# A two-layer decoder trunk on one core: a list scheduler that knows of the DVE/POOL lock, and elementwise work moved from GpSimd to VectorE

## The chip, the core and the metric

The kernel runs on one core of a Trainium2 chip. The engines are named as the profile names them: PE (TensorE; PEld its weight loads), DVE (VectorE), ACT (ScalarE), POOL (GpSimd) and SP (the queue that issues the DMAs). The metric is the device time of one execution in microseconds. The time before is the median of three runs.

## What is computed

`reference()` is a trunk of two layers over 512 tokens of width 1024, all in float32. `c` conditions it: six vectors per layer (shift, scale and gate of the token mixing, then of the MLP) come from one product of `silu(c)` with `w_ada`.

```python
for l in range(DEPTH):
    mod = (ada_in @ w_ada[l] + b_ada[l])[:, None, :]
    sh1, sc1, g1, sh2, sc2, g2 = jnp.split(mod, 6, axis=-1)
    h = x * (1.0 + sc1) + sh1
    proj = h @ w_in[l]
    ...
    o_h = hgrn2(...)          # gated recurrence, 4 heads of 64
    o_n = nsa(...)            # sparse attention, 8 heads in 2 groups
    o_g = gmlp(...)           # chunked spatial gating
    mix = jnp.concatenate([o_h, o_n, o_g], axis=-1) @ w_o[l]
    x = layer_norm(DN_ALPHA * x + (1.0 + g1) * mix, ln1_w[l], ln1_b[l])
    h = x * (1.0 + sc2) + sh2
    y = jnp.square(jax.nn.relu(h @ w_ff1[l])) @ w_ff2[l]
    x = layer_norm(DN_ALPHA * x + (1.0 + g2) * y, ln2_w[l], ln2_b[l])
```

## The kernel before

**Products.** PE multiplies float32 numbers as pairs of rounded float32r parts: each operand is split into a high part (a rounding copy, `whi`) and a low part (the difference, `wlo`), and each product is three matmuls (`mm3`). So every weight tile that a DMA brings (`raw`) costs a copy and a subtraction on ACT, DVE or POOL (`split`), and so does each input tile `hT` (`make_hT`: PE transposes a normalised tile, ACT or DVE multiplies by the scale and adds the shift, then a cast and a difference of 128x256).

**The stretches, by the trace's time.** Layer 0: input projections with the conditioning vectors (0 to 73); gated recurrence, query, key and value projections (73 to 180); compressed keys, attention and the remaining projections (180 to 320); output projection and residual (320 to 398); norm and the MLP's input (398 to 426); MLP (426 to 780); norm and the next layer's input (780 to 808). Layer 1 is the same: recurrence and projections (808 to 920), attention (920 to 1040), output projection (1040 to 1124), norm (1124 to 1152), MLP and end (from 1152).

**Norms.** `layer_norm_rows` gathers statistics on DVE, takes the reciprocal root with two small POOL instructions (`rsqrt`, tile `lnmv`) and normalises in place on DVE. The norm's own weight and bias are folded into the columns `sb` with which `make_hT` makes the next input; the affine rows themselves are needed only much later, as the residual. `affine_rows` (L1623) makes them: per half of the columns and token tile a product and a sum of 128x512 on engine `E`, then a DMA to a scratch tensor `xd`. It is called three times, after ln1 and ln2 of layer 0 and ln1 of layer 1, with `E = G`, which is POOL.

**Conditioning vectors.** `ada_accs` (L906) accumulates `silu(c)[k] * w_ada[k]` over eight k tiles from 512 KB loads. On DVE a step is one fused multiply-add (`scalar_tensor_tensor`); on POOL it is a product into a tile `adat` and a sum. `rest(m, dst, eng)` (L1778) makes the gate `g1` (`ada_row`, two halves) and then shift and scale `sb2` of the MLP (`ada_scale_shift`). Layer 0's are made on POOL (`eng = "G"`), layer 1's on DVE.

**Order.** The program is first written down as a list of operations on virtual tiles. `Plan.schedule` (L332) then places them one by one: per engine a queue of ready operations in order of priority (place in the list plus `plan.shift`), a cost in ns for each (`cost`, L218), latencies between engines, a limited number of tiles of each kind. Many operations have alternatives: `vg` (L765), a product, sum or difference, may go to DVE or, if it has been ready for 500 ns, to POOL; `split` and copies may go to ACT or DVE. The instructions are emitted in the order in which they were placed; engines work through their own instructions in that order. In the trace all instructions have the emitting line, L563, and the tiles of the common pool are all called `t`.

Of the kernel before, what the change touches and what calls it, by code (L numbers as in the profile page):

```python
# [36 lines left out]
# ---------------------------------------------------------------- planning  # L37
# Instructions are first written down with virtual tiles, then placed in time by a
# list scheduler with a rough cost of each instruction, and emitted in that order.
# [117 lines left out]
class Op:  # L157
    __slots__ = ("ahead", "alts", "prio", "seq", "reads", "writes", "succ", "nd", "ready", "vts", "newv", "eng", "end",
# [6 lines left out]
NFILL = 1  # L165
STEPS = (1, 1, 2, 2, 2)
# [22 lines left out]
class Plan:  # L189
# [17 lines left out]
    def limit(self, name, n):  # L207
        """at most n tiles of this name live at once"""
        self.add_class("#" + name, n, 0, None)
        self.lims[name] = "#" + name  # L210
# [6 lines left out]
    # ---- cost in ns  # L217
    def cost(self, eng, method, a, k):  # L218
# [4 lines left out]
        if eng == "PE":  # L223
# [3 lines left out]
            if a[2].dt == F32:  # L227
                return max(2 * n / 2.4, a[1].idx.size / 1.2) + 2 * n / 2.4 + 2.5
            return n / 2.4 + 2.5
# [27 lines left out]
        return 100.0  # L257

    def op(self, alts, also=()):
# [56 lines left out]
        o.nd = len(deps)  # L316
        o.succ = []
# [13 lines left out]
    # ---- placement in time  # L331
    def schedule(self):  # L332
# [7 lines left out]
               "SP": dict(PE=100.0, V=0.0, A=0.0, G=0.0, SP=0.0)}  # L340
        table = None
# [32 lines left out]
        def slot_time(o, t):  # L374
            """earliest time at which the new tiles of o can have slots; INF: not known yet"""
# [29 lines left out]

        for o in self.ops:
            if o.nd == 0:
                push(o)
# [6 lines left out]
        while n_left:  # L415
            best = None
            for e in T:
# [14 lines left out]
                for r in sorted(ready[e])[:200]:  # L432
# [3 lines left out]
                    st = max(slot_time(o, t), bank_time(o, e))  # L436
# [14 lines left out]
                if cand is None:  # L451
                    for r in pend[e]:
# [5 lines left out]
                        fut = min(fut, max(r[0] + (ALT_WAIT if r[2] else 0), slot_time(o, r[0]), bank_time(o, e)))  # L458
# [13 lines left out]
            start = t  # L472
            if e == "PE":
                load = 0.0
                if alt[1] == "matmul":
                    load = alt[2][1].idx.size / (2.4 if alt[2][1].dt == BF else 1.2)
# [30 lines left out]
            if e == "SP":  # L507
# [4 lines left out]
                dma_free = tr + nbytes / 350.0  # L512
                end = dma_free + 950
                T[e] = start + 460
            else:
                end = start + c
                T[e] = end
            o.done = True
# [25 lines left out]
    def place(self, vt):  # L544
        pool, width = self.classes[vt.cls]["pool"], self.classes[vt.cls]["width"]
        n = int(np.prod(vt.shape[1:]))
        t = pool.tile([128, width], vt.dt, name="%s_%d" % (vt.cls, vt.slot), tag="%s%d" % (vt.cls, vt.slot))
# [19 lines left out]
def trunk(ctx: ExitStack, tc: tile.TileContext, I, out, depth=L):  # L567
# [44 lines left out]
    # ------------------------------------------------------------ constants  # L612
# [12 lines left out]
    # ---- condition vector and the bias of its projection, as columns  # L625
# [1214 lines left out]
```

## Time and profile before

| | us |
|---|---|
| median of three runs | 1514.28 |
| lowest, highest | 1511.14, 1516.61 |
| span of the profiled execution | 1509.3 |
| PE busy (share) | 1376.6 (91%) |
| DVE busy | 1170.3 (78%) |
| ACT, POOL busy | 554.9, 462.4 |
| mean granted PE clock | 0.971 |

The span runs from the first to the last instruction of one profiled execution; the median of the runs, taken without the profiler, is 5.0 us above it. Busy time of DVE and POOL counts an instruction from its start to its end, with what it waits for in between at a port. The chain of waits that ended last is 64% PE and 25% DVE.

### The profile page before, as it was taken

The numbers are of one execution on the slowest core, as the hardware profiler recorded it, in microseconds if no ns is written. First come the engines' busy times: TensorE is split into PE (matmuls) and PEld (weight loads), VectorE is DVE, ScalarE is ACT, GpSimd is POOL, SyncE is SP. The second block draws the span as 40 slices with busy tenths as digits, with TensorE's granted clock in tenths as the row PEclk, the third lists the DMA queues.
The fourth block names the chain that finished last, engine by engine and source line by source line (L and its number), as shares of the span: only waits on it lengthen the run. The fifth ranks groups of instructions, "written<-read, shape, count | busy, mean of one in ns | idle before, by whom it ended". The sixth has DMA issues, their size and how long they took to land.

```text
span 1509.3 us, 21620 instructions
## 1 busy us (share of the span) xinstructions
PE 1376.6 (91%) x7459; PEld 1151.8 (76%) x7459; DVE 1170.3 (78%) x2477; ACT 554.9 (37%) x1465; POOL 462.4 (31%) x601
## 2 busy tenths in 40 slices
PE   6867888999879999999998789999896999999996
PEld 4756777777768887888887769888785888888885
DVE  9999979999978557486789995999996663444658
ACT  6541567783203313122314344877421311101121
POOL 6676577453420001010036642223424000000003
PEclk9888999999989999999999899999999999999998
DMA  9521454225466325275414115111454331233331
GB/s 314 183 72 51 119 179 136 71 83 180 152 221 211 132 88 181 97 255 175 147 42 136 35 49 148 30 57 52 147 173 153 126 103 55 94 99 98 111 112 56
DMA packets 119845, 185.69 MB, mean 123 GB/s; under 512 B 9796, under 2 KB 47160, under 8 KB 119736
## 3 DMA queue, kind: packets, MB, share of 16 engines
q1 hardware_dynamic: 119736, 184.31, 38.1%
q8 instruction: 59, 0.97, 0.3%
q14 instruction: 50, 0.41, 0.1%
HBM read 175.89 MB, written 8.39 MB: 122 GB/s over the span
## 4 chain that ended last, share of the span: by engine, by line
PE 64%; DVE 25%; issue 4%; ACT 4%; POOL 2%; DMA 2%; SPq 0%; POOLq 0%; DVEq 0%; ACTq 0%
PE ps L563 64%; DVE t L563 21%; ACT t L563 3%; DVE amax L563 1%; POOL t L563 1%; DMA t<-in_w_ada_dram 1%; DMA raw<-in_w_ada_dram 1%; POOL lnmv L563 1%; DVE acoef L563 1%; DMA t<-in_ln_w_dram 0%; DVE hst L563 0%; POOL hms L563 0%; DVE lt L563 0%; DVE adat L563 0%; POOL gmv L563 0%
## 5 line engine op out<-in xcount | busy, mean ns | idle before, releaser
L563 PE MATMUL ps<-t,t 128*128 128x512 f32 (+5 forms) x6096 | 1261.7, 363 | 72.3 <-DVE t L563 67.2
L563 PEld LDWEIGHTS ps<-t,t 128*128 128x128 f32 x6096 | 1016.5, 193 | 251.8 <-DVE t L563 40.7
L563 ACT ACTIVATE t<-ps 128x512 f32<-128x512 f32 (+11 forms) x462 | 179.0, 413 | 539.9 <-PE ps L563 528.0
L563 POOL TENSOR_TENSOR t<-t,t 128x512 f32<-128x512 f32 (+5 forms) x244 | 241.4, 1004 | 255.4 <-ACT t L563 133.1
L563 DVE TENSOR_TENSOR t<-raw,t 128x512 fp32r<-128x512 f32 (+2 forms) x376 | 248.2, 678 | 13.7 <-ACT t L563 7.2
L563 POOL TENSOR_TENSOR t<-raw,t 128x512 fp32r<-128x512 f32 (+2 forms) x56 | 65.6, 1176 | 535.7 <-ACT t L563 368.5
L563 DVE TENSOR_TENSOR t<-t,t 128x512 fp32r<-128x512 f32 (+6 forms) x270 | 182.2, 694 | 5.9 <-ACT t L563 0.8
L563 DVE TENSOR_TENSOR t<-t 128x512 f32<-128x512 f32 (+1 forms) x94 | 60.1, 653 | 151.7 <-ACT t L563 151.6
L563 ACT ACTIVATE t<-raw 128x512 fp32r<-128x512 f32 (+2 forms) x241 | 128.4, 568 | 129.3 <-DMA raw<-in_w_ff_dram 107.5
L563 PE MATMUL ps<-ident,t 128*128 128x128 f32 (+1 forms) x635 | 110.7, 282 | 36.8 <-DVE t L563 20.4
L563 ACT ACTIVATE t<-t 128x512 fp32r<-128x512 f32 (+5 forms) x202 | 98.1, 510 | 112.0 <-DVE t L563 95.8
L563 PEld LDWEIGHTS ps<-ident,t 128*128 128x128 f32 (+1 forms) x635 | 75.9, 144 | 57.6 <-issue 18.3
L563 DVE TENSOR_TENSOR t<-ps,t 128x512 fp32r<-128x512 f32 (+5 forms) x237 | 109.3, 482 | 9.1 <-ACT t L563 3.9
L563 DVE SCALAR_TENSOR_TENSOR t<-raw,silc,t 128x512 f32<-128x512 f32 x98 | 74.6, 773 | 10.7 <-DMA raw<-in_w_ada_dram 9.4
L563 DVE CAST t<-raw 128x512 fp32r<-128x512 f32 (+2 forms) x191 | 81.4, 430 | 0.2
L563 ACT ACTIVATE t<-ps,amax 128x128 f32<-128x128 f32 (+3 forms) x128 | 67.3, 534 | 20.2 <-DVE amax L563 18.4
L563 DVE TENSOR_TENSOR t<-t,ps 128x512 f32<-128x512 f32 (+1 forms) x48 | 31.1, 650 | 53.7 <-PE ps L563 53.5
L563 DVE TENSOR_REDUCE amax<-ps 128x1 f32<-128x32 f32 (+4 forms) x192 | 65.5, 380 | 4.0 <-PE ps L563 3.1
L563 POOL TENSOR_SCALAR t<-t,acoef 128x384 f32<-128x384 f32 (+3 forms) x55 | 32.2, 599 | 67.6 <-DVE acoef L563 51.7
L563 ACT ACTIVATE t<-ps,adasb 128x256 f32<-128x256 f32 x48 | 23.4, 571 | 72.4 <-PE ps L563 72.4
L563 POOL TENSOR_SCALAR t<-raw,silc 128x512 f32<-128x512 f32 x48 | 37.3, 782 | 27.4 <-PE ps L563 9.9
L563 POOL TENSOR_SCALAR lnmv<-lnmv 128x1 f32<-128x1 f32 x16 | 5.6, 348 | 113.8 <-DVE lnmv L563 113.8
(141 smaller groups left out, 878.5 us busy)
## 6 DMA issues: line engine op xcount, KB each, us to landing
raw<-in_w_ff_dram SPq DMA_DIRECT2D x128, 512.0 KB, 4.5
raw<-in_w_ada_dram SPq DMA_DIRECT2D x80, 512.0 KB, 4.6
raw<-in_w_in_dram SPq DMA_DIRECT2D x49, 256.0 KB, 2.9
t<-in_w_ada_dram SPq DMA_DIRECT2D x32, 256.0 KB, 6.1
raw<-in_w_o_dram SPq DMA_DIRECT2D x16, 512.0 KB, 4.0
raw<-in_w_in_dram SPq DMA_DIRECT2D x15, 512.0 KB, 3.6
xd<-t SPq DMA_DIRECT2D x24, 256.0 KB, 2.2
t<-xd SPq DMA_DIRECT2D x24, 256.0 KB, 4.9
```

Of the source, the lines that this page charges most:

```text
L563: getattr(self.handles[e], method)(*a, **k)
```

## The change

Four things, one of which is the order that follows from the others.

1. The scheduler's `shares` says which instructions of DVE and POOL use the shared port of SBUF: on POOL all but memsets, on DVE those with two SBUF inputs, or with SBUF on both sides of a copy or a scalar operation. `port_time` lets such a DVE instruction start at the earliest 69 ns before the end of POOL's, and POOL's 147 ns before the end of DVE's.
2. Costs: a DVE instruction that needs news from several engines starts 62 ns later for each beyond the first; float32 and float32r matmuls and their weight loads are dearer; DMAs run at 310 instead of 350 bytes per ns.
3. Layer 0's `rest` goes to DVE (`"V"` for `"G"`).
4. `affine_rows` runs on DVE, and its priority is 900 places behind its place in the list, not 250.

Besides, tiles bear their own names in the changed program (`place`), and comments are gone.

```diff
+OPEN_V, OPEN_G = 69.0, 147.0
+WAIT = 62.0
...
             if a[2].dt == F32:
-                return max(2 * n / 2.4, a[1].idx.size / 1.2) + 2 * n / 2.4 + 2.5
-            return n / 2.4 + 2.5
+                return 2 * max(2 * n / 2.4 + 2.5, 111.0)
+            if a[2].dt == BF:
+                return n / 2.4 + 2.5
+            return n / 2.246 + 4.0
...
+    def shares(self, eng, method, a, k):
+
+        if eng == "G":
+            return method not in ("memset", "iota")
+        if eng != "V" or method == "memset":
+            return False
+        out = k.get("out", a[0] if a else None)
+        ins = [x for x in list(a[1:]) + [x for n, x in k.items() if n != "out"] if isinstance(x, VA)]
+        ins = [v for v in ins if v.vt.cls not in self.psum and (v.idx.size > 1 or out.idx.size == 1)]
+        if method in ("tensor_copy", "tensor_scalar"):
+            return bool(ins) and out.vt.cls not in self.psum
+        return len(ins) > 1
...
+        def port_time(o, ai, e):
+            if e not in port or not o.port[ai]:
+                return 0.0
+            return port["G"] - OPEN_V if e == "V" else port["V"] - OPEN_G
...
-                    st = max(slot_time(o, t), bank_time(o, e))
+                    st = max(slot_time(o, t), bank_time(o, e), port_time(o, r[2], e))
...
+            news = 0
+            last = {}
+            for d in o.deps:
+                x, i = d.eng_no
+                last[x] = max(last.get(x, -1), i)
+            for x, i in last.items():
+                if i > seen[e].get(x, -1):
+                    seen[e][x] = i
+                    news += 1
+            if e == "V" and news > 1:
+                start += WAIT * (news - 1)
...
-                    load = alt[2][1].idx.size / (2.4 if alt[2][1].dt == BF else 1.2)
+                    load = 4 + alt[2][1].idx.size / (2.4 if alt[2][1].dt == BF else 1.2)
...
-                dma_free = tr + nbytes / 350.0
+                dma_free = tr + nbytes / 310.0
...
+                if e in port and o.port[ai]:
+                    port[e] = end
...
-        r = layer(l, yn, xd, sb, rest(0, nxt, "G") if l == 0 else iter(()), nxt)
+        r = layer(l, yn, xd, sb, rest(0, nxt, "V") if l == 0 else iter(()), nxt)
         xd = scratch(2 * l)
-        plan.shift = 250
-        affine_rows(r, "ln1_w", "ln1_b", l, xd, G)
+        plan.shift = 900
+        affine_rows(r, "ln1_w", "ln1_b", l, xd, V)
...
-            plan.shift = 250
-            affine_rows(yn, "ln2_w", "ln2_b", l, xd, G)
+            plan.shift = 900
+            affine_rows(yn, "ln2_w", "ln2_b", l, xd, V)
```

The order of the instructions changes on every engine. POOL at the end of layer 0's output projection, where the last two token tiles are normalised (`lnmv`), before; the tiles `t` written from 5151 on are affine rows:

```order
L563 TENSOR_SCALAR lnmv_5158<-lnmv_5158 128x1
L563 TENSOR_TENSOR t_76_5151<-t_76_5151,t_32_5108 128x512
L563 TENSOR_TENSOR lnmv_5158<-lnmv_5158,mhalf 128x1
L563 TENSOR_TENSOR t_54_5187<-t_10_4830,t_61_5098 128x512
L563 TENSOR_TENSOR t_29_5206<-t_14_4863,t_61_5098 128x512
L563 TENSOR_TENSOR t_54_5187<-t_54_5187,t_32_5108 128x512
L563 TENSOR_TENSOR t_29_5206<-t_29_5206,t_32_5108 128x512
```

and in the changed program, from the same normalisation to the splits of the MLP's weights:

```order
L605 TENSOR_SCALAR lnmv_5030<-lnmv_5030 128x1
L605 TENSOR_TENSOR lnmv_5030<-lnmv_5030,mhalf 128x1
L605 TENSOR_SCALAR lnmv_5073<-lnmv_5073 128x1
L605 TENSOR_TENSOR lnmv_5073<-lnmv_5073,mhalf 128x1
L605 TENSOR_TENSOR wlo_5265<-wraw_4600,whi_5237 128x512
L605 TENSOR_TENSOR wlo_5278<-wraw_4600,whi_5257 128x512
```

The sixteen products and sums of the affine rows are no longer there; a part of the MLP's weight splits (`wlo`) takes their place. DVE in layer 0's MLP, where the first sums of the second product are copied out (to `t_52`, `t_70`; `y` in the changed program), before:

```order
L563 TENSOR_TENSOR t_22_5948<-t_14_5940,t_27_5938 128x512
L563 COPY t_52_5954<-ps_5696 128x512
L563 TENSOR_TENSOR t_73_5962<-t_61_5957 128x512
L563 TENSOR_TENSOR t_62_5970<-t_73_5962,t_35_5964 128x512
L563 COPY t_70_5976<-ps_5718 128x512
L563 TENSOR_TENSOR t_79_5981<-raw_5865,t_32_5972 128x512
L563 TENSOR_TENSOR t_50_5991<-raw_5865,t_71_5983 128x512
```

and now:

```order
L605 TENSOR_TENSOR wlo_6107<-wraw_6035,whi_6098 128x512
L605 COPY y_6117<-acc_5898 128x512
L605 COPY y_6136<-acc_5911 128x512
L605 TENSOR_TENSOR xs_6144<-r_4766,lnw_6121 128x512
L605 TENSOR_TENSOR xs_6148<-r_4771,lnw_6121 128x512
L605 TENSOR_TENSOR xs_6144<-xs_6144,lnb_6125 128x512
L605 COPY y_6157<-acc_5924 128x512
```

Products and sums of the affine rows (`xs`) stand there between copies and weight splits; the last of the sixteen comes 41 rows behind the first. The sixteen of layer 0's second norm stand at the start of layer 1's attention, those of layer 1's norm in its MLP. POOL in layer 0's gated recurrence, where the decay differences and products of the levels (64x4x64 and the like) are made, before:

```order
L563 TENSOR_TENSOR t_43_1543<-raw_1281,t_47_1433 128x280
L563 TENSOR_SCALAR t_54_1553<-raw_976,silc 128x512
L563 TENSOR_TENSOR t_66_859<-t_63_1495,t_72_1012 64x4x64
L563 TENSOR_TENSOR t_62_850<-t_9_1499,t_5_996 64x4x64
L563 TENSOR_TENSOR t_64_853<-t_34_1504,t_72_1012 64x4x64
L563 TENSOR_TENSOR t_79_1589<-raw_1353,t_11_1561 128x280
L563 TENSOR_SCALAR t_49_1598<-raw_976,silc 128x512
```

and now:

```order
L605 TENSOR_TENSOR hbd_800<-hx_1285,hgq_916 64x4x64 x2
L605 TENSOR_TENSOR hbd_805<-hx_1331,hgq_931 64x4x64
L605 TENSOR_TENSOR hx_1285<-hx_1285,hgk_956 128x16x16
L605 TENSOR_TENSOR wlo_1513<-wraw_1117,whi_1494 128x512
L605 TENSOR_TENSOR hbd_818<-hx_1292,hgq_916 64x4x64 x2
L605 TENSOR_TENSOR hbd_826<-hx_1335,hgq_931 64x4x64
L605 TENSOR_TENSOR hx_1292<-hx_1292,hgk_956 128x32x8
```

The accumulation steps (`silc`, tile `t_54_1553`) and their sums have left POOL for DVE; the recurrence's products (`hx`, `hbd`) stand there one behind the other, also some that DVE had.

## Rows read from the trace of the kernel before

**Rows 1.** The page's part 1: busy time, share of the span and instructions of each engine.
```profile
PE 1376.6 (91%) x7459; PEld 1151.8 (76%) x7459; DVE 1170.3 (78%) x2477; ACT 554.9 (37%) x1465; POOL 462.4 (31%) x601
```

**Rows 2.** Windows: the stretch, its us, busy us of each engine (instructions), granted clock, DMA share, GB/s.
```profile
0.00:73.00 73.00, 54.12 (x265) 44.78 (x266) 67.12 (x185) 41.09 (x86) 44.73 (x106) 0.91 0.79 245
73.00:180.00 107.00, 78.49 (x476) 67.01 (x475) 100.53 (x222) 44.89 (x124) 69.57 (x80) 0.89 0.28 83
180.00:320.00 140.00, 128.63 (x946) 110.71 (x945) 127.64 (x353) 96.79 (x344) 85.72 (x108) 0.99 0.38 120
320.00:398.00 78.00, 73.50 (x387) 59.18 (x386) 73.62 (x151) 34.76 (x84) 28.89 (x38) 1.00 0.49 159
398.00:426.00 28.00, 14.86 (x115) 13.59 (x114) 25.32 (x29) 5.10 (x11) 24.31 (x21) 0.91 0.26 85
426.00:780.00 354.00, 353.09 (x1566) 287.87 (x1567) 243.63 (x417) 83.77 (x149) 21.74 (x17) 0.99 0.49 163
780.00:808.00 28.00, 20.51 (x150) 19.15 (x148) 25.24 (x26) 5.62 (x12) 25.40 (x25) 0.94 0.31 105
1124.00:1152.00 28.00, 16.19 (x115) 14.17 (x115) 25.99 (x29) 7.40 (x15) 23.34 (x20) 0.93 0.33 115
```

**Rows 3.** Timeline of POOL behind layer 0's first norm: start us, us, what, count.
```profile
403.72 1.29 POOL L563 TENSOR_TENSOR t<-t,t 128x512 f32<-128x512 f32 x1
405.47 19.37 POOL L563 TENSOR_TENSOR t<-t,t 128x512 f32<-128x512 f32 x14
```

**Rows 4.** Groups by shape, 405 to 425, DVE: busy us, mean ns, idle before.
```profile
L563 DVE TENSOR_TENSOR t<-t,t 128x256 fp32r<-128x256 f32 x7 | 9.0, 1315 | 0.0
L563 DVE CAST t<-t 128x256 fp32r<-128x256 f32 x7 | 8.2, 1209 | 0.0
```

**Rows 5.** Timeline of DVE, just before and just after POOL's long run.
```profile
397.97 0.28 DVE L563 CAST t<-t 128x256 fp32r<-128x256 f32 x1
425.05 0.68 DVE L563 TENSOR_TENSOR t<-raw,t 128x512 fp32r<-128x512 f32 x1
425.65 0.41 DVE L563 TENSOR_TENSOR t<-t,t 128x256 fp32r<-128x256 f32 x1
```

**Rows 6.** Timeline of PE: the first full-rate products of layer 0's MLP.
```profile
425.78 2.50 PE L563 MATMUL ps<-t,t 128*128 128x512 f32 x5 [8.45 <-DVE t L563]
```

**Rows 7.** Timeline of POOL behind layer 1's first norm.
```profile
1132.51 17.59 POOL L563 TENSOR_TENSOR t<-t,t 128x512 f32<-128x512 f32 x13
```

**Rows 8.** Groups by shape over the whole span.
```profile
L563 DVE TENSOR_TENSOR t<-ps,t 128x512 fp32r<-128x512 f32 x88 | 56.4, 681 | 1.1 <-PE ps L563 0.6 <-ACT t L563 0.2
L563 POOL TENSOR_TENSOR t<-t,t 128x512 f32<-128x512 f32 x105 | 142.8, 1378 | 100.5 <-ACT t L563 86.5 <-DVE t L563 9.7 <-PE ps L563 3.0
L563 POOL TENSOR_TENSOR t<-t,t 128x256 f32<-128x256 f32 x49 | 40.6, 833 | 44.7 <-DVE t L563 33.2 <-ACT t L563 10.5
L563 POOL TENSOR_SCALAR t<-raw,silc 128x512 f32<-128x512 f32 x48 | 37.3, 782 | 27.4 <-PE ps L563 9.9 <-DMA raw<-in_w_ada_dram 8.4 <-DVE t L563 3.4
L563 ACT ACT_TABLE_LOAD x12 | 15.4, 1283 | 7.7 <-DVE t L563 6.7 <-PEq L1828 0.8
```

**Rows 9.** Groups by shape, 73 to 180, DVE.
```profile
L563 DVE TENSOR_TENSOR t<-t,t 128x256 f32<-128x256 f32 x18 | 15.6, 882 | 0.2
L563 DVE TENSOR_TENSOR t<-t,t 64x256 f32<-64x256 f32 x17 | 14.4, 862 | 0.2
```

**Rows 10.** Groups by shape, 808 to 920, DVE.
```profile
L563 DVE TENSOR_TENSOR t<-t,t 64x256 f32<-64x256 f32 x15 | 13.0, 874 | 0.1
```

**Rows 11.** Instructions of tile raw on DVE, 426 to 745: min/median/max ns; idle us before it, times.
```profile
L563 DVE SCALAR_TENSOR_TENSOR t<-raw,silc,t x70: 734/750/1672, 426.5 to 683.0; 128x512 f32<-128x512 f32 x70
  DMA raw<-in_w_ada_dram: 10.7, 11
```

**Rows 12.** Chain that ended last, in order of time: start us, us, what.
```profile
556.86 3.94 DMA raw<-in_w_ada_dram
566.48 5.83 DMA raw<-in_w_ada_dram
```

More of the change, by code (lines that the diff above doesn't have):

```diff
@@ L157 @@
 class Op:
-    __slots__ = ("ahead", "alts", "prio", "seq", "reads", "writes", "succ", "nd", "ready", "vts", "newv", "eng", "end",
+    __slots__ = ("ahead", "alts", "port", "deps", "eng_no", "prio", "seq", "reads", "writes", "succ", "nd", "ready", "vts", "newv", "eng", "end",
                  "tabs", "banks", "done")
@@ L316, in op @@
         o.nd = len(deps)
+        o.deps = list(deps)
         o.succ = []
@@ L340, in schedule @@
                "SP": dict(PE=100.0, V=0.0, A=0.0, G=0.0, SP=0.0)}
+        count = {e: 0 for e in T}
+        seen = {e: {} for e in T}
         table = None
@@ L404, in bank_time @@
             return max([vt.bank_end for vt in o.banks if vt.bank_eng != e], default=0.0)
+        def port_time(o, ai, e):
+            if e not in port or not o.port[ai]:
+                return 0.0
+            return port["G"] - OPEN_V if e == "V" else port["V"] - OPEN_G
         for o in self.ops:
+            o.port = [self.shares(*alt) for alt in o.alts]
             if o.nd == 0:
@@ L457, in schedule @@
                             continue
-                        fut = min(fut, max(r[0] + (ALT_WAIT if r[2] else 0), slot_time(o, r[0]), bank_time(o, e)))
+                        fut = min(fut, max(r[0] + (ALT_WAIT if r[2] else 0), slot_time(o, r[0]), bank_time(o, e),
+                                           port_time(o, r[2], e)))
                     if fut < INF:
@@ L472, in schedule @@
             start = t
+            o.eng_no = (e, count[e])
+            count[e] += 1
+            news = 0
[9 more added lines that the diff above has]
+                start += WAIT * (news - 1)
             if e == "PE":
@@ L546, in place @@
         n = int(np.prod(vt.shape[1:]))
-        t = pool.tile([128, width], vt.dt, name="%s_%d" % (vt.cls, vt.slot), tag="%s%d" % (vt.cls, vt.slot))
+        t = pool.tile([128, width], vt.dt, name="%s_%d" % (vt.name, vt.slot), tag="%s%d" % (vt.cls, vt.slot))
         ap = t[:vt.shape[0], :n]
```

## The prediction

> **What bounds the kernel now.** First the page's sums [rows 1]: PE is busy for 1376.6 of 1509.3 us, DVE for 1170.3. A mean over stages with different limits decides nothing, so I read the trace stretch by stretch [rows 2]. In the MLP (426 to 780) PE is busy for 353.09 of 354 us: nothing can be won there. In 73 to 180 (the gated recurrence and the key and value projections of layer 0) PE has 78.49 of 107 us and DVE 100.53: DVE sets the pace. The same goes for the three short stretches behind a norm, 398 to 426, 780 to 808 and 1124 to 1152, where DVE and POOL are both busy for 23 to 26 of 28 us and PE for 14.86, 20.51 and 16.19.
>
> Next, what DVE is busy with there. Behind the first norm POOL runs 14 affine products and sums of 128x512 in one go, 19.37 us, and a product of 1.29 us just ahead of the reciprocal root that the last normalisation waits for [rows 3]. In the same time DVE's casts and differences of 128x256 that make the MLP's input take 1209 and 1315 ns each [rows 4]; with POOL quiet they take 0.28 and 0.41 us [rows 5]. Each waits for a POOL instruction of 1.38 us. PE stands idle for 8.45 us in front of its next full-rate product, released by DVE [rows 6]. The other two norms look the same, with 13 POOL instructions in one go each; the row of the third, 17.59 us, stands for both [rows 7]. What reads PSUM doesn't suffer: the difference with one PSUM input takes 681 ns on the mean of 88, like the 0.68 us of one from SBUF with POOL quiet [rows 5, 8]. So a part of DVE's busy time is waiting for POOL, wherever both work from SBUF. In 73 to 180 the products of 128x256 and 64x256 take 882 and 862 ns [rows 9] instead of 0.41 us: 18 x 0.47 + 17 x 0.45 = 16 us of waiting in two groups alone. In 808 to 920 the one of 64x256 stands at 874 [rows 10]: 15 x 0.46 = 7 us.
>
> **The change, part by part.**
>
> *Affine rows.* 3 x 16 POOL instructions (1378 ns on the mean of that shape [rows 8]) leave the stretches behind the norms and become 48 DVE instructions of about 0.69 us, some 900 places later: those of the first and last norm in the MLPs, those of the middle one at the start of layer 1's attention, as the order shows. First norm: DVE gets back 7 x (1.209 - 0.28) + 7 x (1.315 - 0.41) = 12.8 us [rows 4, 5] and 1.29 us on the root [rows 3]: 14 us. PE has only 28 - 14.9 = 13.1 us of room, and must still wait for transposes and the first cast: I take 11 of it. Second norm: the room is 28 - 20.5 = 7.5, but DVE carries on from there, so 8. Third: room 11.8, taken 10. Sum **-29**; ends -19 (two thirds) and -36. The new 48 cost DVE 33 us. In the MLP DVE has 354 - 244 = 110 us free, so 11 us there cost nothing; without that cover they would be paid in full (third rival).
>
> *Layer 0's gate, shift and scale.* POOL loses 48 products of 782 ns and 42 sums (16 + 32 products; all but the first of each of 6 accumulators is added) at 1378 ns [rows 8]: 37.5 + 57.9 = 95 us. DVE gains 48 instructions at about 750 ns [rows 11], 36 us, and the split of two gate halves. Up to the last row maximum of layer 0's attention the order nevertheless has 722 DVE instructions where 755 stood: some 80 leave DVE, mostly products, differences and sums of 128x256 and 64x256, nearly all for POOL, which has 285 where 295 stood. At 0.41 us those 80 are 33 us, so DVE's own work stays level, and POOL's falls by about 95 - 80 x 0.83 = 29 of 200 us.
>
> *The scheduler.* It now knows that POOL and DVE shut each other out, charges DVE for each further semaphore, and has slower loads. This changes the order, not the work. In 73 to 180 I take half of the 16 us of waiting, **-8**: POOL's recurrence products are still there, but they stand in one long run beside DVE's PSUM work. Ends: -16 (all), +9 (first rival). In 808 to 920 **-7**, ends -12 (7 and as much again in smaller groups, less what overlaps) and +12. In 0 to 73 the DMA share is 0.79 [rows 2] and the loads are the same: **-3**, ends 0 and -8. In 180 to 320, from which most of the POOL accumulation goes, PE's room is 140 - 128.6 = 11.4 us: half, **-6**, ends +5 and -11. Output projections, 320 to 398 and its like in layer 1: **-2** each, PE being busy for 73.5 of 78. ScalarE has 15 table loads instead of 12, at 1283 ns [rows 8], mostly beside other work: **+2**. MLPs and the tail: 0.
>
> Sum: -29 - 8 - 7 - 3 - 6 - 4 + 2 = **-55 us**. The profiled execution's span is 1509.3 us, 5.0 under the median of 1514.28, which I take for what lies around it: the span goes to 1454, the median to **1459 us**.
>
> **Rivals.**
>
> *The moved products hold the lock twice as long.* A 128x256 product takes 0.83 us on POOL [rows 8] and 0.41 on DVE. In 73 to 180 the order gives POOL 13 instructions more, in 808 to 920 and its surroundings 31. If what both engines take from SBUF has to go one after the other, and that is the bound, these stretches grow by 13 x 0.42 = 5 and 31 x 0.4 = 12 us instead of shrinking by 8 and 7: -55 + 15 + 17 = -23, **1491**. For it: in 73 to 180 POOL's 69.57 us and the two groups of DVE products from SBUF, 30.0 us with their waiting [rows 2, 9], make 100 of the 107 us. Against it: DVE's order there is filled with work from PSUM, which runs beside POOL at full speed [rows 8]. The Trainium skill ("SBUF — State Buffer", SBUF: two separate sides) states the lock in just this form: exclusive, held for the whole instruction, and only against DVE instructions in a two-port mode or with two SBUF inputs. By that rule the two stretches would not shrink and the time would be this rival's; the trace agrees with the lock itself, but not that the sum is the bound, since DVE and POOL together are busy for 170 us in those 107. Chance 0.17.
>
> *Slower: DVE's queue stands still behind weight loads.* The 48 units need 24 loads of 512 KB. On POOL, which nobody awaited, a late load cost nothing; on DVE everything behind it waits, the recurrence and PE with it. In the MLP this happens: two such waits stand in the chain, 3.94 and 5.83 us [rows 12]. If each of the 24 cost their mean, 4.9, that would be +117, **1576**; it decides from 55 / 24 = 2.3 us per load. Against it: DVE idled only 10.7 us in 11 waits for such loads in the whole first MLP, with 70 such units [rows 11], and DMA is less busy here (0.28 and 0.38 in 73 to 320, 0.49 there [rows 2]). Chance 0.08.
>
> *The MLP pays.* The affine rows stand on DVE between the weight splits that feed PE. If PE has to wait for all of them, 33 us come back: -22, **1492**. Against it: DVE's 110 free us. Chance 0.07.
>
> **Numbers.** Forecast 0.68, rivals 0.17, 0.08 and 0.07. The forecast's own range is 1425 to 1488: with every end at its best the sum is -85, 1429, and the clock granted in 73 to 180, 0.89 [rows 2], may rise once PE waits less; with the norms at -19 and the rest at a third it is -26, 1488. To take in the first and third rival the 8-in-10 range reaches to 1503. A measurement of this kernel tells about 0.3%, 4.5 us, from no change. Faster by more: the forecast, the first rival and most of the third, less what two rivals together would undo, 0.87. Slower: the second rival and a little of that, 0.09. Within: 0.04.
>
> **What would show it.** Behind each norm, casts and differences of 128x256 near 0.3 and 0.4 us, no POOL run of 13 or 14, and PE's idle time before its first full-rate product under 2 us: this step alone should bring the first matmul of the MLP some 11 us nearer to the norm. In 73 to 180, products of 128x256 on DVE well under 0.88 us and a shorter stretch; if they fall but the stretch doesn't, the lock sum is the bound (first rival). DVE idle before accumulation units, released by DMA, in layer 0's first 320 us would show the second rival; PE idle in the MLP, released by DVE, the third. The prediction is wrong if the three norm stretches stay near 28 us, or if PE's idle time moves from there to another place.

## The result, and the profile after

The changed kernel takes **1458.77 us** (median of 4 runs, 1456.48 to 1461.59), the kernel before 1514.41 in the same session: a ratio of 0.9635, 95% interval 0.9618 to 0.9652, so 55.6 us less. The profiled execution's span is 1456.9 us against 1509.3, which is 52.4 less. In the runs of the changed kernel the span stands 1.7 us below the run's time; the 1509.3 before stands 5.0 us below its median. So the trace before is most likely that of one of the shorter executions (the shortest took 1511.14), and the other 3 us are spread between executions, not a gain outside the span.

The page after, parts 1 and 2 (the last line is the granted clock in 40 slices of 36 us), to be read against [rows 1]:

```profile
PE 1376.1 (94%) x7459; PEld 1162.9 (80%) x7459; DVE 1102.2 (76%) x2361; ACT 580.6 (40%) x1516; POOL 444.8 (31%) x631
...
PEclk9888999999999999999999995999999999999999
```

PE's work is what it was; DVE's busy time fell by 68 us. One slice of the clock stands out, from 874 to 910 us: 5 among nines. It comes back below. The windows after, cut at the places that answer to [rows 2] (columns as there):

```profile
68.00:168.00 100.00, 74.17 (x486) 67.17 (x485) 92.27 (x238) 53.36 (x130) 72.02 (x93) 0.87 0.26 77
168.00:307.00 139.00, 133.27 (x965) 117.30 (x964) 119.78 (x333) 97.81 (x350) 53.13 (x88) 0.96 0.42 128
...
381.00:397.00 16.00, 16.00 (x120) 15.05 (x119) 14.07 (x40) 8.55 (x20) 4.98 (x7) 1.00 0.34 108
397.00:747.00 350.00, 348.78 (x1563) 283.79 (x1562) 244.44 (x395) 90.16 (x160) 33.46 (x24) 1.00 0.51 169
747.00:765.00 18.00, 17.76 (x131) 16.56 (x130) 15.77 (x41) 7.63 (x17) 6.26 (x14) 1.00 0.00 1
...
870.00:1008.00 138.00, 134.45 (x884) 118.32 (x883) 109.31 (x307) 93.30 (x342) 44.02 (x77) 0.88 0.25 73
...
1083.00:1103.00 20.00, 19.58 (x139) 17.98 (x138) 19.32 (x43) 9.20 (x22) 6.52 (x8) 1.00 0.30 95
```

Behind the norms PE is now busy for 16.00 of 16, 17.76 of 18 and 19.58 of 20 us, where it had 14.86, 20.51 and 16.19 of 28. The reason shows in DVE's groups by shape, 376 to 397, after:

```profile
L605 DVE TENSOR_TENSOR hT<-hf,hT 128x256 fp32r<-128x256 f32 x14 | 5.3, 420 | 0.0
L605 DVE CAST hT<-hf 128x256 fp32r<-128x256 f32 x14 | 3.7, 289 | 0.9 <-ACT hf L605 0.7
```

and in POOL's timeline there, which holds no affine row any more (it idles 5.98 us up to its next weight split):

```profile
390.49 0.55 POOL L605 TENSOR_TENSOR lnmv<-lnmv,mhalf 128x1 f32<-128x1 f32 x1
397.02 3.33 POOL L605 TENSOR_TENSOR wlo<-wraw,whi 128x512 fp32r<-128x512 f32 x2 [5.98 <-ACT whi L605]
```

The casts and differences that took 1209 and 1315 ns [rows 4] take 289 and 420, what they took with POOL quiet [rows 5]; and the affine product of 1.29 us that stood between the two instructions of the last reciprocal root [rows 3] is gone (the root's own product takes 0.55 us now, 0.54 before).

To compare stretches that start and end at other times in each kernel, I cut every trace at the same events: the first gate tile of a layer's recurrence (`hgk`), the last value tile, the last residual row `r` of the output projection, the last tile of the next input (`hT`), the last activation of the MLP. In us:

| stretch | before | after |
|---|---|---|
| A: up to layer 0's first gate | 72.5 | 67.8 |
| B: recurrence and key/value projections | 107.2 | 100.1 |
| C: attention and output projection (by the last row maximum) | 139.3 + 89.4 | 139.5 + 84.6 |
| D: first norm | 17.6 | 5.1 |
| E: MLP to its last activation | 309.2 | 310.6 |
| F: end of MLP, middle norm, to layer 1's first gate | 79.6 | 69.4 |
| G: layer 1, recurrence + attention + output projection | 103.2 + 122.1 + 95.2 | 92.1 + 138.4 + 88.0 |
| H: layer 1's first norm | 16.4 | 7.4 |
| I: MLP and end | 354.0 | 350.7 |

One part goes clearly the wrong way: layer 1's attention takes 16.3 us more.

### The profile page after: what moved, and what is told of

The parts are those of the page before. It is cut to its first block, busy times and chain, and to the rows that moved or that the text cites. A ratio compares the mean times of both kernels' runs of the same rounds, so it can differ in the third digit from the quotient of the medians.

```text
span 1456.9 us, 21608 instructions
## 1 busy us (share of the span) xinstructions
PE 1376.1 (94%) x7459; PEld 1162.9 (80%) x7459; DVE 1102.2 (76%) x2361; ACT 580.6 (40%) x1516; POOL 444.8 (31%) x631
## 4 chain that ended last, share of the span: by engine, by line
PE 47%; DVE 9%; POOL 3%; DMA 2%; issue 2%; ACT 2%; POOLq 0%; DVEq 0%; ACTq 0%; SPq 0%
PE acc L605 39%; PE aps L605 4%; PE ps L605 3%; DVE rt L605 1%; DMA adaw<-in_w_ada_dram 1%; DVE xs L605 1%; DVE y L605 1%; DMA wraw<-in_w_ff_dram 1%; DVE lnst L605 1%; DVE adacc L605 1%; POOL lnmv L605 1%; DVE wlo L605 1%; ACT KV L605 1%; DVE hT L605 1%; DVE amax L605 0%
## 5 line engine op out<-in xcount | busy, mean ns | idle before, releaser
L605 PE MATMUL acc<-hT,whi 128*128 128x512 f32 (+1 forms) x1296 | 415.1, 375 | 5.4 <-ACT hT L605 3.4
L605 PE MATMUL acc<-whi,aT 128*128 128x512 f32 x896 | 325.3, 395 | 0.0
L605 PEld LDWEIGHTS acc<-hT,whi 128*128 128x128 f32 x1296 | 236.5, 191 | 51.3 <-ACT hT L605 4.2
L605 PE MATMUL acc<-hT,wlo 128*128 128x512 f32 (+1 forms) x648 | 239.8, 373 | 1.3 <-DVE wlo L605 1.3
L605 PE MATMUL acc<-whi,hT 128*128 128x256 f32 (+2 forms) x1024 | 232.0, 312 | 2.2 <-DVE qs L605 1.5
L605 DVE TENSOR_TENSOR wlo<-wraw,whi 128x512 fp32r<-128x512 f32 (+2 forms) x299 | 205.0, 703 | 13.1 <-ACT whi L605 7.5
L605 PEld LDWEIGHTS acc<-whi,aT 128*128 128x128 f32 x896 | 168.2, 188 | 39.5
L605 PEld LDWEIGHTS acc<-whi,hT 128*128 128x128 f32 x1024 | 170.8, 193 | 8.8 <-issue 1.2
L605 PE MATMUL acc<-wlo,aT 128*128 128x512 f32 x448 | 176.8, 395 | 0.3 <-DVE wlo L605 0.3
L605 PE MATMUL acc<-wlo,hT 128*128 128x256 f32 (+2 forms) x512 | 158.4, 310 | 0.0
L605 DVE SCALAR_TENSOR_TENSOR adacc<-adaw,silc,adacc 128x512 f32<-128x512 f32 x140 | 108.3, 786 | 23.6 <-DMA adaw<-in_w_ada_dram 22.1
L605 ACT ACTIVATE P<-aps,amax 128x128 f32<-128x128 f32 (+3 forms) x128 | 67.3, 531 | 12.7 <-DVE amax L605 11.1
```

The lines of the kernel that those rows point to most:

```text
L605: getattr(self.handles[e], method)(*a, **k)
```

## Experiments

All were timed in three rounds against the kernel before on the same chip; a ratio stands with its 95% interval.

### The affine rows alone

The kernel before, with this edit (it, the next and the fourth also name tiles as the changed kernel does):

```diff
-        plan.shift = 250
-        affine_rows(r, "ln1_w", "ln1_b", l, xd, G)
+        plan.shift = 900
+        affine_rows(r, "ln1_w", "ln1_b", l, xd, V)
...
-            plan.shift = 250
-            affine_rows(yn, "ln2_w", "ln2_b", l, xd, G)
+            plan.shift = 900
+            affine_rows(yn, "ln2_w", "ln2_b", l, xd, V)
```

> The kernel before with one part of the change: the affine rows on DVE, 900 places later; old scheduler, layer 0's gate on POOL. Theory A (POOL's lock behind the three norms holds up the MLP's input, and the place behind a norm is where it counts): 25 to 35 us faster than before, 1480 to 1490, each of the three norm stretches some 10 us shorter, the rest as before. Theory B (the scheduler's new rules make nearly all of the 55 us; the affine rows moved little by themselves): 1500 to 1510. Theory C (only all parts together pay, since an old order gives the gain back elsewhere): within 5 us of before.

Measured: 1476.09 us, 0.9754 (0.9729 to 0.9778), 39 less. D, F and H fall from 17.6, 79.6 and 16.4 to 5.1, 68.8 and 6.4: 33.3 us in the three norm stretches, close to the 29 forecast for them. C falls by another 4.5, A and B rise by 2.5.

### The gate, shift and scale alone

```diff
-        r = layer(l, yn, xd, sb, rest(0, nxt, "G") if l == 0 else iter(()), nxt)
+        r = layer(l, yn, xd, sb, rest(0, nxt, "V") if l == 0 else iter(()), nxt)
```

> The kernel before with one part of the change: layer 0's gate, shift and scale on DVE; old scheduler, affine rows on POOL. Theory A: POOL loses 95 us and DVE gains 36 in a part where DVE sets the pace, less waiting makes up for it: between 5 us faster and 5 slower than before, 1509 to 1519. Theory B: the same. Theory D (the queue of DVE stands still behind weight loads unless the scheduler knows better): 10 us or more slower, 1525 and above, with DVE idle before its accumulation steps.

Measured: 1511.96 us, 0.9987 (0.9970 to 1.0003), no difference. 95 us taken from POOL bring nothing by themselves under the old scheduler.

### The scheduler alone

The changed kernel's scheduler and costs, with both moves undone:

```diff
-        r = layer(l, yn, xd, sb, rest(0, nxt, "V") if l == 0 else iter(()), nxt)
+        r = layer(l, yn, xd, sb, rest(0, nxt, "G") if l == 0 else iter(()), nxt)
...
-        plan.shift = 900
-        affine_rows(r, "ln1_w", "ln1_b", l, xd, V)
+        plan.shift = 250
+        affine_rows(r, "ln1_w", "ln1_b", l, xd, G)
```

(and the same for the middle norm.)

> The changed kernel with both moves undone: new scheduler (lock, costs), affine rows on POOL 250 places later, layer 0's gate on POOL. Theory A: the scheduler avoids waiting in the recurrences but must still put 16 POOL instructions behind each norm or delay them itself: 12 to 30 us faster than before, 1485 to 1502. Theory B: 40 us or more faster, below 1475. Theory C: within 5 us of before.

Measured: 1471.69 us, 0.9725 (0.9700 to 0.9749), 43 less: more than I had thought the scheduler worth. It shortens the norms by itself (D 9.0, F 73.6, H 6.5) although POOL still makes the affine rows there. But B, the stretch in which I had looked for its gain, becomes longer: 115.8 instead of 107.2. The three parts alone sum to 39 + 3 + 43 = 85 us; together they bring 55.6. They aren't independent.

### The affine rows on POOL, only later

```diff
-        plan.shift = 250
+        plan.shift = 900
         affine_rows(r, "ln1_w", "ln1_b", l, xd, G)
```

(the kernel before, and the same for the middle norm.)

> The kernel before with the affine rows still on POOL, but 900 places later; old scheduler. If the place matters (they hold the lock behind the norm, where the MLP's input waits) and not the engine: as fast as the affine rows on DVE alone, within 6 us of that run, the norm stretches some 10 us shorter. If the engine matters (1.38 us on POOL for 0.69 on DVE, wherever they stand, hold up DVE): half of that gain or less, with DVE's casts and differences in the MLP lengthened and PE waiting for weight splits there.

Measured: 1481.27 us, 0.9785 (0.9756 to 0.9815), 34 less; D, F and H are 5.1, 68.9 and 5.3, as with the rows on DVE. So what counted behind the norms was the place of these instructions, not the engine. What is left between the two engines, 5 us, is within the intervals.

### The changed kernel without the lock rule

```diff
-            if e not in port or not o.port[ai]:
-                return 0.0
+            return 0.0
```

> The changed kernel, but the scheduler's port_time always returns 0, so that it places DVE's and POOL's instructions as if they didn't shut each other out; the new costs (waits, loads, matmuls) and both moves stay. Theory A: what the scheduler wins comes from knowing the lock; without it DVE's products in 68 to 168 and its casts wait for POOL again, and the time goes up by 8 to 20 us: 1467 to 1479. Theory B: the dearer costs alone make the better order, since nearly all POOL work behind the norms is gone already: 1450 to 1463.

Measured: 1485.12 us, 0.9807 (0.9780 to 0.9834), 26 more than the changed kernel and more than either theory gave. The new costs without the lock rule are, if anything, worse than the old ones: the old scheduler with the affine rows alone stood at 1476. By the cuts the loss lies mostly in the output projection of layer 0 (94.8 instead of 84.6), in B (108.3 instead of 100.1), in G (324.3 instead of 318.5) and in I (356.3 instead of 350.7). What PE waited for in the whole span (us in all, times, longest) shows the recurrence's products among it:

```profile
PE ps L604 <- DVE hx L604: 17.1, 6, 8.6
PE ps L604 <- POOL hx L604: 9.2, 6, 4.5
```

In the changed kernel the first of the two is 4.7 us, and one wait for the query's rotation (shown further down) takes 21.5. The first theory's reason does not hold, though: in B, DVE's products wait for POOL no more without the rule than with it (71 to 179; the changed kernel's groups stand further down):

```profile
L604 DVE TENSOR_TENSOR hbd<-hx,hgq 64x256 f32<-64x256 f32 x18 | 13.4, 752 | 0.2
...
L604 DVE TENSOR_TENSOR hx<-hx,hgk 128x256 f32<-128x256 f32 x13 | 8.0, 631 | 0.1
...
L604 DVE TENSOR_TENSOR hx<-hb 128x256 f32<-128x256 f32 x10 | 5.4, 590 | 0.0
```

What the rule changes is how the work is shared: with it DVE has 2361 instructions instead of 2511 and is busy for 1102.2 us instead of 1157.3, POOL has 631 instead of 518. That the rule wins is shown; that it wins by shorter waits at the lock is not.

### The lock rule with the old costs

```diff
-WAIT = 62.0
+WAIT = 0.0
...
-                return 2 * max(2 * n / 2.4 + 2.5, 111.0)
+                return max(2 * n / 2.4, a[1].idx.size / 1.2) + 2 * n / 2.4 + 2.5
...
-                dma_free = tr + nbytes / 310.0
+                dma_free = tr + nbytes / 350.0
```

> The changed kernel with the scheduler's knowledge of the lock and both moves, but with all the costs as they were before (no 62 ns per further semaphore, the old matmul, weight load and DMA costs). Theory A: it is the lock alone that wins, since without it and with the new costs the time is 1485, above the affine rows alone (1476); the new costs then win nothing: 1445 to 1465. Theory B: the lock rule and the costs need each other (an engine placed too early makes the lock's windows wrong): 1468 to 1485.

Measured: 1462.85 us, 0.9664 (0.9641 to 0.9687); the intervals of this and of the changed kernel overlap. As the first theory had it, the scheduler's gain is that of the lock rule; the costs add nothing that can be told here. How much the rule is worth depends on what it is set against: with the new costs 26 us (the run above), with the old ones some 13, if the old scheduler with the affine rows alone (1476) is taken for the kernel without it. Both moves together were not run under the old scheduler.

### The changed kernel with the affine rows back on POOL, 250 places later

The edit of the first experiment, reversed, in the changed kernel.

> The changed kernel with the affine residual rows back on POOL and 250 places later, as they were; the scheduler and layer 0's gate, shift and scale on DVE stay. Theory A: the new scheduler holds the affine rows' POOL instructions apart from DVE's casts by itself, so the two parts overlap: as the scheduler alone (1471.7) or a little better, 1465 to 1475. Theory B: the parts add up, the norm stretches go back to some 28 us each and the gain of the affine rows alone (38 us) is lost in full: 1490 to 1500.

Measured: **1451.13 us**, 0.9593 (0.9566 to 0.9620), below both theories and 8 us below the changed kernel, though the intervals just touch. Once the scheduler knows the lock, moving the affine rows wins nothing. POOL's timeline behind the first norm in this kernel (start us, us, what) shows why:

```profile
389.58 1.34 POOL L605 TENSOR_TENSOR xs<-xs,lnb 128x512 f32<-128x512 f32 x1
390.88 2.75 POOL L605 TENSOR_TENSOR xs<-r,lnw 128x512 f32<-128x512 f32 x2
393.59 4.73 POOL L605 TENSOR_TENSOR hT<-hf,hT 128x256 fp32r<-128x256 f32 x5
398.28 3.46 POOL L605 TENSOR_TENSOR xs<-xs,lnb 128x512 f32<-128x512 f32 x2
```

POOL breaks off its affine rows (`xs`) for five of the differences that make the MLP's input, 0.95 us each, and takes the rows up again when PE has its input. Before, 14 rows stood there in one go [rows 3]. D is 7.1 us with them, 5.1 without.

### The changed kernel with gate, shift and scale back on POOL

The edit of the second experiment, reversed, in the changed kernel.

> The changed kernel with layer 0's gate, shift and scale back on POOL (95 us of POOL work); the scheduler and the affine rows on DVE stay. Theory A: that work is hidden beside other work on either engine, as it was with the old scheduler, where it made no difference: 1455 to 1465, and the stage lengths of layer 0 within 4 us. Theory B: under the lock-aware scheduler 95 us of POOL's instructions shut DVE out in layer 0's first 320 us, or the scheduler pushes them to where they are late: 1468 to 1490.

Measured: 1470.00 us, 0.9725 (0.9699 to 0.9750), 11 more than the changed kernel: the second theory's lower end. B is 115.8 us, as with the scheduler alone, instead of 100.1. So the move that is worth nothing under the old scheduler is worth 15.7 us of B under the new one; elsewhere it gives some of it back (G is 312.3 with the accumulations on POOL, against 318.5). PE's waits (who waited for what, us in all, times, longest) with the scheduler alone, 66 to 182:

```profile
PE ps L605 <- DVE qrope L605: 34.7, 1, 34.7
```

and after, 68 to 168:

```profile
PE ps L605 <- DVE qrope L605: 21.5, 1, 21.5
```

This one wait, for the query's rotation on DVE, makes 13.2 of the 15.7 us (with gate, shift and scale back on POOL it is 34.7 too). In that stretch POOL, with the scheduler alone, has these groups beside the recurrence:

```profile
L605 POOL TENSOR_TENSOR adacc<-adacc,adat 128x512 f32<-128x512 f32 x11 | 14.7, 1336 | 0.4
...
L605 POOL TENSOR_SCALAR adat<-adaw,silc 128x512 f32<-128x512 f32 x9 | 8.2, 915 | 0.0
```

22.9 us of POOL's accumulations, which by the lock rule the scheduler must place apart from DVE's products. That they are what delays the rotation is the reading that fits; which of the products gave way to them was not tried.

### Keys and compression blocks held on DVE

In the changed kernel PE idles 0.91, 0.60 and 1.00 us for POOL's sums just ahead of layer 1's compression (the products that shorten keys and values, `ps<-cblk,cw`), and then the clock falls. PE's timeline after:

```profile
869.40 0.44 PE L605 MATMUL ps<-ident,krope 128*128 128x128 f32 x2 [0.91 <-POOL krope L605]
...
876.40 0.44 PE L605 MATMUL ps<-ident,krope 128*128 128x128 f32 x2 [0.60 <-POOL krope L605]
...
878.09 3.31 PE L605 MATMUL ps<-cblk,cw 128*128 128x62 f32 x22 [1.00 <-POOL cblk L605]
```

The same stretch in windows, after (the column behind the engines is the granted clock):

```profile
868.00:880.00 12.00, 9.30 (x77) 8.40 (x75) 11.57 (x39) 5.40 (x23) 11.00 (x20) 1.00 0.60 206
880.00:892.00 12.00, 12.00 (x58) 12.00 (x58) 6.46 (x12) 1.50 (x4) 5.96 (x8) 0.50 0.68 205
892.00:904.00 12.00, 12.00 (x58) 12.00 (x58) 1.75 (x7) 1.25 (x6) 0.00 (x0) 0.50 0.45 126
```

So I held the sums on DVE, in the changed kernel:

```diff
-                gv("tensor_add", dst.rearrange("p (h r d) -> p h r d", r=2, d=64)[:, :, r], d3, t[:, :nh])
+                V.tensor_add(dst.rearrange("p (h r d) -> p h r d", r=2, d=64)[:, :, r], d3, t[:, :nh])
...
-            gv("tensor_add", d3, d3, t[:, :nh])
+            (gv if nh == 4 else lambda m, *z: V.tensor_add(*z))("tensor_add", d3, d3, t[:, :nh])
...
-                    vg("tensor_add", blk[:, :, g, :], kv[:, a0:a0 + 7:2, n0:n0 + NBLK], pec)
+                    V.tensor_add(blk[:, :, g, :], kv[:, a0:a0 + 7:2, n0:n0 + NBLK], pec)
```

> The changed kernel with the key rotation's sums (krope) and the sums that fill the compression blocks (cblk) held on DVE instead of being open to POOL; nothing else is touched. Theory A: in layer 1 PE idles 0.91, 0.60 and 1.00 us for these POOL sums just ahead of the compression products, the granted clock then falls to 0.5 and the 128 products take 26 us instead of 14.6, with the rest of that dip on the products behind them. With the sums on DVE PE doesn't wait, the clock holds, and layer 1's attention takes 116 to 124 us instead of 138: 1437 to 1447. Theory B: the dip has nothing to do with who writes those tiles; it stays there or moves to a neighbouring place, the stretch stays at 130 to 140 us: 1455 to 1465.

Measured: 1452.45 us, 0.9605 (0.9585 to 0.9624). The compression products by group, busy us and mean ns, before (918 to 942):

```profile
L563 PE MATMUL ps<-t,raw 128*128 128x62 f32 x128 | 14.6, 275 | 0.0
```

after (866 to 906):

```profile
L605 PE MATMUL ps<-cblk,cw 128*128 128x62 f32 x128 | 26.1, 403 | 1.0 <-POOL cblk L605 1.0
```

and with the sums on DVE (866 to 905):

```profile
L605 PE MATMUL ps<-cblk,cw 128*128 128x62 f32 x128 | 14.8, 275 | 0.0
```

The dip is gone, and with it 11 us of these products. But layer 1 from its first gate to its last residual takes 316.7 us, against 318.5; the 6 us that this kernel wins lie elsewhere, mostly in C of layer 0 (217.2 instead of 224.1). My theory was half wrong: the dip followed on who writes those tiles, but the stretch had another bound, and what PE no longer lost to the clock it lost to waiting (PE busy 290.83 of 317 us, against 303.87 of 319).

### The middle norm's rows alone back on POOL

The chain of waits after, 860 to 900 (start us, us, what), shows what PE waited for: affine rows (`xs`) on DVE, then POOL's sums.

```profile
867.43 0.60 DVE xs L605
869.48 0.60 DVE xs L605
870.18 0.78 DVE xs L605
870.99 0.85 DVE xs L605
...
877.18 0.87 POOL cblk L605 x2
878.09 22.09 PE ps L605 x110
```

They are the middle norm's, 16 instructions on DVE between 854.8 and 881.9, ahead of what the compression wants from DVE; a moment later POOL too waits for one of them before its next block (its timeline):

```profile
879.86 2.35 POOL L605 TENSOR_TENSOR cblk<-KV,pecol 128x124 f32<-128x124 f32 x3 [1.00 <-DVE xs L605]
```

The edit, in the changed kernel:

```diff
-            plan.shift = 900
-            affine_rows(yn, "ln2_w", "ln2_b", l, xd, V)
+            plan.shift = 250
+            affine_rows(yn, "ln2_w", "ln2_b", l, xd, G)
```

> The changed kernel with the affine rows of the middle norm alone back on POOL, 250 places later, as before; those of layer 0's and layer 1's first norm stay on DVE, 900 places later. Theory A: the middle rows are what costs layer 1 its time: with them on DVE the stretch from the norm to layer 1's residual takes 318.5 us (with the dip) or 316.7 (keys on DVE, without), with them on POOL 306. So that stretch falls to 302 to 310, the middle norm's grows by some 4 (as with all rows on POOL): 1444 to 1454. Theory B: the slow stretch is a matter of the order's details, not of these rows; it stays at 314 to 322: 1456 to 1468.

Measured: 1450.12 us, 0.9583 (0.9563 to 0.9603), whose interval lies wholly below the changed kernel's. G falls from 318.5 to 305.7, F rises from 69.4 to 73.6, both as the first theory had it.

### The middle norm's rows on POOL, but still 900 places later

```diff
-            affine_rows(yn, "ln2_w", "ln2_b", l, xd, V)
+            affine_rows(yn, "ln2_w", "ln2_b", l, xd, G)
```

> The changed kernel with the affine rows of the middle norm alone on POOL, still 900 places later. Theory A (the engine): on DVE these 16 instructions stand between 854.8 and 881.9, in the recurrence's end and the first blocks of the compression, where DVE is wanted; on POOL at the same place they don't hold DVE up, the middle norm keeps its short 57 us and layer 1 falls to some 306: 1442 to 1450. Theory B (the place): POOL's instructions there shut DVE out for twice as long and stand ahead of POOL's own sums for the compression (krope, cblk): layer 1 stays at 314 to 326, 1455 to 1467.

Measured: **1446.01 us**, 0.9554 (0.9533 to 0.9574), the lowest of this study, though its interval overlaps those of the run above and the run below. F keeps its 69.4, G falls to 311.5: not as far as to the 306 that I named, but below the second theory's 314 to 326. That is 7.0 us in G; the rest of the gain is spread over other stretches. POOL's eight pairs start there between 847.0 and 871.7, and the trace names nothing that waited for them.

### The middle norm's rows on DVE, 1600 places later

```diff
-            plan.shift = 900
+            plan.shift = 1600
             affine_rows(yn, "ln2_w", "ln2_b", l, xd, V)
```

> The changed kernel with the affine rows of the middle norm on DVE, 1600 places later instead of 900, which moves them on DVE from rows 1383 to 1450 of its order to rows 1471 to 1525, behind the blocks of the compression. Theory A (the place on DVE): freed of them, the recurrence's end and the compression run as with the middle rows on POOL early, without a dip at the compression; the middle norm stays short: 1440 to 1450. Theory B: DVE pays the same 11 us wherever in layer 1's attention they stand: 1453 to 1462.

Measured: 1449.35 us, 0.9577 (0.9559 to 0.9595), within the first theory's range. The same instructions on the same engine start 41 us later (896.1 to 923.8), behind the compression, which here runs from 871.85 to 886.29: G is 308.7. The windows of this kernel, to be read beside those after:

```profile
868.00:880.00 12.00, 11.26 (x100) 11.06 (x100) 9.85 (x39) 3.31 (x15) 7.08 (x16) 1.00 0.55 168
880.00:892.00 12.00, 12.00 (x112) 11.77 (x112) 3.58 (x20) 5.08 (x26) 0.73 (x1) 1.00 0.46 133
```

PE has 11.26 instead of 9.30 us of work in front of the compression, the clock holds, and 112 instead of 58 products go through in the next 12 us. So three edits that clear DVE between 855 and 882 of these 16 instructions (another engine early, another engine at the same place, the same engine later) each win 9 to 13 us by the medians, 8 to 12 by the ratios.

All of these edits reorder the rest too, so I set G side by side for the nine kernels that have the lock rule:

| middle norm's rows | G, us |
|---|---|
| DVE, 900 places later | 318.5 (changed kernel), 316.7 (keys on DVE), 312.3 (gate, shift and scale on POOL), 324.4 (old costs) |
| POOL, 250 places later | 305.5 (scheduler alone), 306.0 (all rows on POOL), 305.7 (middle rows alone) |
| POOL, 900 places later | 311.5 |
| DVE, 1600 places later | 308.7 |

The four with the rows in that place on DVE are the four slowest, if only by 0.8 us. So that the place costs layer 1 time agrees with every run; how much is not shown, since with the rows in the same place G still spreads over 12 us by other details of the order, and the run with the keys on DVE won 6 us in all without moving the rows. Nor is it separated how much is the clock and how much the wait ahead of it: without the dip, keys on DVE lost as much to waiting. Under the old scheduler the same 900 places cost nothing there: G is 320.5 before and 320.7 with the affine rows alone moved.

## Why the prediction was right, and where it was not

The total was right, 1459 forecast and 1458.8 measured. That it is right to the microsecond is luck: it came by terms that were off on both sides, and the 5.0 us that I added to the span for what lies around it measured 1.7 (a span of 1454 forecast, 1456.9 measured). So I go through the terms. Forecast and measured, in us:

| term | forecast | measured |
|---|---|---|
| norms (D, F, H) | -11, -8, -10 | -12.5, -10.2, -9.0 |
| output projections | -2, -2 | -4.8, -7.2 |
| 73 to 180 (B) | -8 | -7.1 |
| 180 to 320 | -6 | +0.2 |
| layer 1's recurrence | -7 | -11.1 |
| layer 1's attention | 0 | +16.3 |
| 0 to 73 | -3 | -4.7 |
| MLPs and tail (E, I) | 0 | +1.4, -3.3 |
| table loads | +2 | in the stretches above |
| sum | -55 | -52.0 |

**What bounds, and the affine rows.** Right, mechanism and size: casts and differences returned to the times that [rows 5] gave, PE's idle time behind the norms is gone, and the rows alone take 33.3 us from the three stretches. What the step missed is that the scheduler alone would have done most of that (D 9.0, F 73.6, H 6.5). So the sum named the right 32 us, but the changed kernel doesn't owe them to the move alone: with the lock rule in force, undoing the move makes it no slower (1451).

**Gate, shift and scale; 180 to 320.** Here the step failed. I took half of that stretch's room, 6 us, for the accumulations that leave POOL, and got nothing (+0.2); with the accumulations back on POOL that stretch even takes 132.0 us instead of 139.5. Their worth was in B, 15.7 us, and only under the new scheduler.

**73 to 180.** The number was right for the wrong reason. I gave the 8 us to the scheduler; the scheduler alone costs 8.6 there, and the move of the accumulations gives back 15.7. DVE's groups of that stretch after, against [rows 9]:

```profile
L605 DVE TENSOR_TENSOR hbd<-hx,hgq 64x256 f32<-64x256 f32 x9 | 7.2, 806 | 1.3 <-ACT hx L605 1.2
L605 DVE TENSOR_TENSOR hx<-hb 128x256 f32<-128x256 f32 x11 | 7.1, 701 | 0.0
...
L605 DVE TENSOR_TENSOR hx<-hx,hgk 128x256 f32<-128x256 f32 x5 | 4.0, 816 | 0.1
```

The first and the last, with two different tiles to read, answer to [rows 9]: at 806 and 816 ns they still wait, hardly less than the 862 and 882 before, but there are 14 where 35 stood, the rest on POOL. The middle one reads one tile twice; before, its like was this group (73 to 180):

```profile
L563 DVE TENSOR_TENSOR t<-t 128x256 f32<-128x256 f32 x15 | 7.1, 507 | 0.0
```

It waits more now, 701 instead of 507 ns. The lock wasn't avoided here, its load was shared out otherwise; the sign that I had named, products of 128x256 of [rows 9] well under 0.88 us, didn't come (816 ns).

**Layer 1's attention.** The step that failed most. I noted that the middle norm's rows land at the start of layer 1's attention and costed them at nothing there; the cover that I named, DVE's free 110 us, was the MLP's. In front of the compression DVE had none: 11.57 of 12 us busy from 868 to 880. Some of those 16 instructions stand in the chain ahead of PE's waits, the clock fell to 1.2 GHz and stayed there for the compression, and the three runs that move them away win 9 to 13 us in all and 7.0 to 12.8 us in G. Layer 1 from its first gate to its last residual fell by only 2.0 us, where I had forecast 9. The sign that I had named, PE's idle time in another place, would hardly have told: from 870 to 1008 PE is busy for 134.45 of 138 us, but at a granted clock of 0.88.

**The rivals.** The first, that products moved to POOL hold the lock twice as long and that the sum bounds B, did not come about in the changed kernel, where B shrank. With the accumulations on POOL as well B did grow, by 8.6 us against the 5 that this rival gave, with POOL busy for 86.03 of 116 us; so the stretch can grow, and the part of the change that I had costed in another stretch is what averted it. That the sum of both engines' work bounded it there is not shown: of the 15.7 us by which it is longer than in the changed kernel, 13.2 are the one wait for the query's rotation. The rule of the Trainium skill ("SBUF — State Buffer", SBUF: two separate sides), that the loser is shut out for the whole instruction, agrees with the casts' 1209 ns beside POOL and 289 without. The second rival fell: in layer 0, with 48 accumulation steps on DVE, its waits for their weights were these (tile `adacc` on DVE, 0 to 310, after; us, times):

```profile
  DMA adaw<-in_w_ada_dram: 4.3, 3
```

instead of 4.9 us for each of 24 loads. The third fell as well: PE in layer 0's MLP waited 1.2 us in all for DVE's weight splits, and E grew by 1.4. That nothing can be won in the MLP, as I had put it, is not so, however: with the scheduler alone E is 304.7 instead of 309.2, for a reason that no run here shows.

## What to carry to other kernels

Where two engines shut each other out, first make the planner know it: that was worth 26 us here (1485 without, 1459 with; some 13 with the old costs), and it made a move by hand worth nothing that under the old planner had won 39. It won by another division of the work, not by shorter waits of DVE in the recurrence. Parts of a change that relieve the same wait don't add up, and some win only together, as the accumulations did; so price each part against the schedule that the others leave. When work is put off to get it out of a critical stretch, price the place where it lands as carefully as the place that it leaves: 900 places later lay the next tight stretch under the new schedule (under the old one the same place cost nothing), and 1600 places later, or the slower engine at the same place, was 9 to 13 us better.

## What the runs showed of the hardware

After idle times of 0.91, 0.60 and 1.00 us (PE busy for 9.30 of 12 us), the granted clock fell from 1.00 to 0.50, that is to 1.2 GHz, at 879.9 us, and stayed there for 34.1 us, through two windows in which PE was busy for 12.00 of 12 us. The 128 products of the compression took 403 ns each on the mean instead of 275, 26.1 us instead of 14.6 in the kernel before. The clock came back behind them, among other products. The price was a dozen microseconds of product time for 2.5 us of waiting, at a place where the whole of PE's queue stood behind these products. What that is worth in the kernel's time is not shown: the run without the dip had 1.8 us less in G, because PE waited there instead.
